# A gMLP mixer's seven products: where the low parts are made and when the additions are issued

## The chip, the cores and the metric

The kernel runs on one core of a Trainium2 chip. The metric is the device time of one execution in microseconds, given as the median of several runs.

## The reference

A trunk of two layers over 512 frames of 1024 channels in float32. Each layer is a half-step SwiGLU FFN, a mixer, a second half-step FFN and a gated input embedding; each step is followed by a LayerNorm. Layer 0's mixer is an mLSTM, layer 1's is the gMLP of which this document speaks:

```python
def gmlp_mixer(x, w_in, b_in, vn_g, vn_b, ws, bs, w_out):
    B, S, _ = x.shape
    NB = S // GM_BLOCK
    u, v = jnp.split(jax.nn.gelu(x @ w_in + b_in, approximate=False), 2, axis=-1)
    v = layer_norm(v, vn_g, vn_b).reshape(B, NB, GM_BLOCK, GM_GROUPS, GM_GDIM)
    blk = jnp.arange(GM_BLOCK) // CHUNK
    mask = blk[:, None] >= blk[None, :]
    ws_m = jnp.where(mask, ws, jnp.zeros((), ws.dtype))
    s = jnp.einsum('gts,bnsgc->bntgc', ws_m, v) + bs.T[:, :, None]
    return (u * s.reshape(B, S, GM_WIDTH)) @ w_out
```

u and v have 2048 columns each. The part that the change touches computes v: 512 frames by 1024 channels times 1024 x 2048 weights, GELU, and the statistics of v's LayerNorm.

## The kernel before

**Three matmuls per product.** Every float32 operand is split in two: a high part, rounded to fp32r, and a low part, the rest. A product is three matmuls (high x high, low x high, high x low): lines L432, L433 and L434 (`mm3`).

**Weights.** The class `Weights` (W) has one list of weight tiles, in the order in which PE takes them, each 128x1024. `load` brings raw weights from HBM over SP's queue (L265) into raw slots; two half-size loads can share a slot, a "box". `fill` goes down the list as far as tiles of the next one's kind ("main": four, "extra": two) are free, and makes the high part on ACT (L311) and the low part in one of two ways: on DVE by a subtraction (L318), or, for the forms named in `by_dma`, by a negated copy on ACT (L306) to which POOL's queue adds the source by an accumulating DMA (L307). `release` gives a tile's place back, at once (and fills) or, with `later=True`, into a list `held` from which `refill(n)` takes n. Fills are thus issued at the places in the program where `release` and `refill` stand. The list order, and with it each engine's instruction order, is written out by hand; an engine takes its instructions strictly in that order and waits where an operand or a buffer isn't ready. A new tile in a buffer waits for every use of the old one, also for uses that stand further down in the program.

**v's columns** are made in chunks of 512. Chunk 2 is plain: `plain(2)` goes over four blocks of 128 tokens, each 24 matmuls into one PSUM bank (`gvps`), then DVE adds the bias (L1756), ACT applies GELU (L1716) and DVE takes the statistics (L1720). Hooks in blocks 1 and 2 turn the last 256 tokens of the layer's input (transposes, xh on ACT, xl on DVE, L705). Chunk 3 is done likewise at the end, `plain(3)`, with the scales of the LayerNorm.

**Chunks 0 and 1** together are done by a seven-product scheme (Strassen-Winograd) over halves of tokens and columns, in two halves of the inner dimension: products r = 0 to 6, each 24 matmuls, whose weights are seven forms:

```python
        made = [((b11[0],), as_loaded(b11)), ((b21[0],) if by_dma else (b12[0], b22[0], b21[0]), as_loaded(b21)), ((b12[0], b22[0]) if by_dma else (), t2),
                ((), t1), ((), as_loaded(b12)), ((), as_loaded(b22)), ((), as_loaded(b21))]
```

Form 2 (`t2`) and form 3 (`t1`) are sums made in place on DVE, `t2` of one sum after `t3`, which `sum_early` issues ahead, and `t1` of two (L134, L135); each stands twice, once for each half of the inner dimension. The other side's forms come from the input: u, w, y and z hold sums of token halves, `in_forms(r, f)` and `in_place(r, f)` split them for product r (the second in one buffer, tag "hp"). Products alternate between two pairs of PSUM banks, `banks[r % 2]`; `adds(r)` adds a pair to v on DVE (L1822) with the bias where it is the first, and must be done before product r + 2 starts, since that writes to the same pair. `adds(5)` and `adds(6)` also give the pairs back to `plain(3)`. `run_affine` finishes the LayerNorm before the mixer, for the residual: a multiplication on DVE (L820) and an accumulating DMA (L822), one for each of four token blocks. `load_spatial` loads `gm_ws` over ACT's queue (L1681); it is transposed on PE (L1691) after `plain(3)`'s first token block.

## Time and profile before

| what | us |
|---|---|
| median of 3 runs | 2194.47 (2193.58 to 2194.95) |
| the profiled execution's own time | 2195.17 |
| its span in the profile | 2193.3 |
| PE busy in the span | 2162.9 |
| first matmul of the chunk `plain(2)` | at 1488.1 |
| first matmul of the spatial sums, after `plain(3)` | at 1601.0 |

Times within the span are counted from its start. PE, PEld, DVE, ACT and POOL are TensorE's matmuls, its weight loads, VectorE, ScalarE and GpSimd; SPq, ACTq and POOLq are DMA issues. A row in order of time gives start and duration, the engine and the line, output <- inputs, and in brackets how long the engine had been idle and what ended that. A row of waits gives the total, the number of times and the longest.

### The profile page before, as it was taken

To read this page: it belongs to the slowest core of one execution; us is meant where nothing else is said; L and a number is where in the kernel's file an instruction comes from. 1 tells how busy PE (TensorE), PEld (TensorE's weight loads), DVE (VectorE), ACT (ScalarE), POOL (GpSimd) and SP (SyncE) were. 2 spreads that over 40 slices of the span, in tenths; PEclk is the share of its full clock that TensorE was granted. 3 is DMA by queue.
4 is the path that set the end of the run, shared out by engine and by line. 5 is a ranking of instruction groups with operands and counts; after the bars stand their busy time and mean duration, and the time that the engine had idled before them with its cause. 6 is when DMAs were issued, how large, how long until landed. Compare 5 with 4: busy or idle time off the path is not lost.

```text
span 2193.3 us, 33288 instructions
## 1 busy us (share of the span) xinstructions
PE 2162.9 (99%) x13085; PEld 1931.4 (88%) x13085; DVE 1775.8 (81%) x2551; ACT 1263.7 (58%) x1733; POOL 259.7 (12%) x315
## 2 busy tenths in 40 slices
PE   9999999999999999999999999998799999999998
PEld 8999998888888889999888999997688888999987
DVE  6988878777776789888878988887578788888887
ACT  4666656364646556666445666655555555666542
POOL 1111101020111111111001111100101101111100
PEclk9999999999999999999999999999899999999999
DMA  7787764375747487776536787753847738777651
GB/s 217 180 195 188 174 172 113 85 159 131 163 111 154 116 205 179 176 186 159 163 111 168 184 201 188 169 146 90 220 102 134 165 116 221 181 183 180 140 173 58
DMA packets 233478, 348.40 MB, mean 159 GB/s; under 512 B 9908, under 2 KB 164660, under 8 KB 233320
## 3 DMA queue, kind: packets, MB, share of 16 engines
q0 software_dynamic: 57408, 119.73, 32.3%
q1 hardware_dynamic: 169296, 211.83, 29.8%
q10 hardware_dynamic: 6616, 14.69, 2.0%
q8 instruction: 103, 1.69, 0.3%
q14 instruction: 55, 0.45, 0.1%
HBM read 224.58 MB, written 2.11 MB: 103 GB/s over the span
## 4 chain that ended last, share of the span: by engine, by line
PE 41%; DVE 4%; DMA 2%; ACT 2%; issue 2%; POOL 0%; SPq 0%; ACTq 0%; DVEq 0%; POOLq 0%
PE ups L434 5%; PE ups L433 5%; PE ups L432 5%; PE gps L432 4%; PE gps L433 4%; PE gps L434 4%; PE dps L432 1%; PE dps L434 1%; PE dps L433 1%; PE gups L432 1%; PE gups L433 1%; PE gups L434 1%; PE fps L434 1%; PE fps L432 1%; PE fps L433 1%
## 5 line engine op out<-in xcount | busy, mean ns | idle before, releaser
L311 ACT ACTIVATE whi<-wbox 128x1024 fp32r<-128x1024 f32 x266 | 278.7, 1053 | 231.2 <-DVE wbox L159 100.6
L433 PE MATMUL ups<-xl,whi 128*128 128x256 f32 x1152 | 326.0, 283 | 0.0
L434 PE MATMUL ups<-xh,wlo 128*128 128x256 f32 x1152 | 326.0, 283 | 0.0
L432 PE MATMUL ups<-xh,whi 128*128 128x256 f32 x1152 | 325.8, 283 | 0.0
L307 POOL DMA_DIRECT2D wlo<-wbox x160 | 136.0, 850 | 1000.5 <-ACT wlo L306 650.1
L432 PE MATMUL gps<-whi,fhi 128*128 128x512 f32 x644 | 252.9, 393 | 0.0
L433 PE MATMUL gps<-wlo,fhi 128*128 128x512 f32 x644 | 252.3, 392 | 0.0
L434 PE MATMUL gps<-whi,flo 128*128 128x512 f32 x644 | 251.5, 391 | 0.0
L311 ACT ACTIVATE whi<-wraw 128x1024 fp32r<-128x1024 f32 (+1 forms) x188 | 192.5, 1046 | 102.3 <-DVE wraw L135 22.6
L433 PEld LDWEIGHTS ups<-xl,whi 128*128 128x128 f32 x1152 | 220.6, 191 | 2.6
L432 PEld LDWEIGHTS ups<-xh,whi 128*128 128x128 f32 x1152 | 220.6, 191 | 2.6
L434 PEld LDWEIGHTS ups<-xh,wlo 128*128 128x128 f32 x1152 | 220.6, 192 | 0.0
L831 DVE TENSOR_TENSOR xt<-xt,gps 128x512 f32<-128x512 f32 x302 | 195.6, 682 | 28.8 <-PE gps L434 28.6
L306 ACT ACTIVATE wlo<-wbox 128x1024 fp32r<-128x1024 f32 x160 | 167.2, 1045 | 11.4 <-DVE wbox L167 11.4
L318 DVE TENSOR_TENSOR wlo<-wraw,whi 128x1024 fp32r<-128x1024 f32 (+1 forms) x111 | 132.6, 1213 | 47.7 <-ACT whi L311 46.9
L311 ACT ACTIVATE whi<-wquarter 128x1024 fp32r<-128x1024 f32 (+1 forms) x140 | 135.2, 966 | 58.6 <-ACT wlo L306 20.4
L434 PEld LDWEIGHTS gps<-whi,flo 128*128 128x128 f32 x644 | 120.9, 188 | 26.9
L432 PEld LDWEIGHTS gps<-whi,fhi 128*128 128x128 f32 x644 | 121.3, 188 | 22.0
L433 PEld LDWEIGHTS gps<-wlo,fhi 128*128 128x128 f32 x644 | 121.4, 188 | 21.3
L324 DVE TENSOR_TENSOR wlo<-wquarter,whi 128x1024 fp32r<-128x1024 f32 (+1 forms) x116 | 139.2, 1200 | 0.0
L1020 DVE TENSOR_TENSOR flo<-h,fhi 128x512 fp32r<-128x512 f32 (+1 forms) x140 | 89.0, 636 | 46.1 <-ACT fhi L1017 45.8
L324 DVE TENSOR_TENSOR wlo<-wbox,whi 128x1024 fp32r<-128x1024 f32 x92 | 112.2, 1219 | 0.0
(413 smaller groups left out, 5826.9 us busy)
## 6 DMA issues: line engine op xcount, KB each, us to landing
wlo<-wbox POOLq DMA_DIRECT2D x160, 512.0 KB, 5.6
wbox<-in_ffn_wgu_dram SPq DMA_DIRECT2D x144, 512.0 KB, 4.9
wquarter<-in_ffn_wd_dram SPq DMA_DIRECT2D x64, 512.0 KB, 6.5
wraw<-in_ml_w_in_dram SPq DMA_DIRECT2D x24, 1024.0 KB, 5.9
wlo<-wraw POOLq DMA_DIRECT2D x48, 512.0 KB, 6.5
wraw<-in_gm_w_in_dram SPq DMA_DIRECT2D x11, 1024.0 KB, 6.6
wraw<-in_ffn_wgu_dram SPq DMA_DIRECT2D x17, 512.0 KB, 5.6
wraw<-in_ffn_wd_dram SPq DMA_DIRECT2D x8, 1024.0 KB, 5.5
```

The source lines that it names most:

```text
L306: self.nc.scalar.activation(lo[:, s], src[:, s], AF.Copy, scale=-1.0)
L307: self.nc.gpsimd.dma_start(lo[:, s], src[:, s], accum_op=OP.add)
L311: self.nc.scalar.activation(hi[:, s], src[:, s], AF.Copy)
L318: self.nc.vector.tensor_sub(lo[:, s], src[:, s], hi[:, s].bitcast(F32))
L324: self.nc.vector.tensor_sub(lo, src, hi.bitcast(F32))
L432: mm(ps, st[0], mv[0], start=start, stop=False, skip_group_check=more)
L433: mm(ps, st[0], mv[1], start=False, stop=False, skip_group_check=more)
L434: mm(ps, st[1], mv[0], start=False, stop=stop, skip_group_check=more)
L831: vec.tensor_add(dst, dst, ps)
L1020: vec.tensor_sub(lo, src, hi.bitcast(F32))
```

## The change

- Form 0's low parts are also made by accumulating DMA, and for all of these forms the negated copy goes ahead of the high part.
- Ahead of `plain(2)`, all loads that have room are issued and `fill` runs, so that both tiles of form 0 are made there.
- In `plain(2)`: after block 0 the sums of z and y; after block 1 `sum_early` and, by `form_ahead(4, True)`, both sums `t2`; after block 2 the input's sums and three held statistics; in block 3 the splits for product 2, a refill and the high part of the input of product 3. Three tiles are released at once there, where it was two.
- Within the products, after the first half of product r: `adds(r - 1)` stands first, and behind it form sums, refills, splits, statistics and affine steps. Both sums `t1` stand in a row behind `adds(0)`. Tiles are released later and taken back by `refill`.
- The affine steps move from products 2 to 5 to products 4, 5 (two) and 6; `load_spatial` moves from the end of product 5 into product 6, behind its refill; chunk 3's bias load moves into product 5. The statistics of chunks 0 and 1 move behind later additions, the last ones behind `adds(6)`.

```diff
-V_BY_DMA = (1, 4, 5, 6)
+V_BY_DMA = (0, 1, 4, 5, 6)
...
+        self.neg_first.update(made[r][1] for r in by_dma)
         return [(kind, js, make) for js, make in made]
...
-                if by_dma and make in self.sums:
+                neg_first = make in self.sums or make in self.neg_first
+                if by_dma and neg_first:
                     negated()
                 self.nc.scalar.activation(hi[:, s], src[:, s], AF.Copy)
...
-                if by_dma and make not in self.sums:
+                if by_dma and not neg_first:
                     negated()
...
-    def form_ahead(self, n):
+    def form_ahead(self, n, now=False):
...
-                if self.loaded_at[j] > self.clock - 2:
+                if not now and self.loaded_at[j] > self.clock - 2:
                     return
...
-                if c >= 2:
+                if c == 3:
                     stats()
+                elif c == 2:
+                    held_stats.append(stats)
                 return stats
...
-                    W.release(later=len(given) >= (2 if c < 3 else 1))
+                    W.release(later=len(given) >= (3 if c < 3 else 1))
...
             def first_tokens():
-                W.sum_early()
                 for e, s in enumerate(halves):
                     vec.tensor_add(z[e], *(a[:, s].bitcast(F32) for a in quarters[0]))
-
-            def more_tokens():
                 vec.tensor_add(y, *(a.bitcast(F32) for a in quarters[1]))
 
+            def weight_sums():
+                W.sum_early()
+                W.form_ahead(4, True)
+
...
             def in_place(r, f):
                 both = hpool.tile([P, 2, 4, 256], F32R, name="x_s", tag="hp")
                 for s, src in f:
-                    split(both[:, 0, s], both[:, 1, s], src)
-                left[r] = both[:, 0], both[:, 1]
+                    sca.activation(both[:, 0, s], src, AF.Copy)
+                left[r] = both[:, 0], both[:, 1]
+
+                def low():
+                    for s, src in f:
+                        vec.tensor_sub(both[:, 1, s], src, both[:, 0, s].bitcast(F32))
+                return low
...
-            ahead = lambda: W.form_ahead(4)
-            plain(2, vbs[0], (((), (first_tokens,)), ((), (more_tokens,)),
-                              ((sums,), (lambda: W.form_ahead(4),)), ((lambda: in_forms(2, z),), ())))
-            banks, add, stats = [], lambda: None, lambda: None
+            while W.load():
+                pass
+            W.fill()
+            third_low = []
+            plain(2, vbs[0], (((), (first_tokens,)), ((), (weight_sums,)), ((), (sums, lambda: [held_stats.pop(0)() for _ in range(3)])),
+                              ((lambda: in_forms(2, z), W.refill, lambda: third_low.append(in_place(3, [(slice(0, 4), w)]))), ())))
+            banks = []
...
-                return take(j, (2 * i, 2 * i + 1)) if r in (1, 4, 5, 6) else lambda: None
+                return lambda: take(j, (2 * i, 2 * i + 1))
...
-                    if k == 0 and r:
-                        stats()
-                        stats = adds(r - 1)
-                    W.release()
-                    if r == 1 and k == 0:
-                        in_place(3, [(slice(0, 4), w)])
-                    elif r == 1:
-                        fourth_sum()
+                    if k == 0:
+                        if r == 0:
+                            new_v(0)
+                        elif r == 1:
+                            adds(0)
+                            W.form_ahead(2)
+                            W.refill(2)
+                            third_low[0]()
+                        elif r == 2:
+                            gelus = adds(1)
+                            in_forms(4, [u[:, s] for s in halves])
+                            held_stats.append(gelus())
+                            fourth_sum()
+                            new_v(1)
+                        elif r == 3:
+                            adds(2)
+                            in_place(5, list(zip(halves, z)))()
+                            held_stats.pop(0)()
+                        elif r == 4:
+                            adds(3)
+                            held_stats.pop(0)()
+                            run_affine(1, True)
+                        elif r == 5:
+                            held_stats.append(adds(4)())
+                            W.refill(2)
+                            next_vb = load_bias(3)
+                            run_affine(2, True)
+                        else:
+                            held_stats.append(adds(5)())
+                            W.refill(2)
+                            load_spatial()
+                            held_stats.pop(0)()
+                            run_affine(1, True)
+                    W.release(later=True)
+                    if k == 1 and r in (1, 2, 3):
                         W.refill(2)
                 W.clock += 2
-                if r in (0, 2):
-                    new_v(r // 2)
-                if r == 2:
-                    in_forms(4, [u[:, s] for s in halves])
-                elif r == 3:
-                    in_place(5, zip(halves, z))
-                elif r == 5:
-                    load_spatial()
-                    next_vb = load_bias(3)
-                if 2 <= r <= 5:
-                    run_affine(1, True)
-            stats()
-            adds(6)()
+            last = adds(6)()
+            for stats in held_stats:
+                stats()
+            last()
             new_v(3)
```

More of the change, by code (lines that the diff above doesn't have):

```diff
@@ L68, in __init__ @@
         self.boxes, self.rank, self.loaded_at, self.clock = [], {}, {}, 0
-        self.lent, self.early = None, []
+        self.lent, self.early, self.neg_first = None, [], set()
         self.hold, self.limit, self.ahead, self.forced, self.sums = False, None, False, False, set()
@@ L1712, in load_bias @@
                 return vb
+            held_stats = []
             def take(c, ts):
```

## The prediction

> **What bounds the kernel now.** I read the page first, then who PE waited for, then a table of stages around the change, then the engines' instructions in order of time.
>
> ```profile
> span 2193.3 us, 33288 instructions
> PE 2162.9 (99%) x13085; PEld 1931.4 (88%) x13085; DVE 1775.8 (81%) x2551; ACT 1263.7 (58%) x1733; POOL 259.7 (12%) x315
> ...
> PE gvps L432 <- DVE gvf L1822: 12.8, 3, 7.9
> PE gvps L433 <- DMA wlo<-wbox: 2.8, 1, 2.8
> PE gvps L434 <- DVE xl L705: 1.8, 1, 1.8
> PE gvps L432 <- DVE gvf L1756: 1.0, 1, 1.0
> ```
>
> TensorE sets the time: the kernel ends when PE has worked through its list, so only PE's waits and its clock can be won. The four lower rows are PE's waits (total, times, longest) in the gMLP's v: 18.4 us. The stages (length, PE busy, PEld, DVE, ACT, POOL, granted clock, DMA share, GB/s):
>
> ```profile
> 1512.00:1532.00 20.00, 16.14 (x57) 12.43 (x56) 16.79 (x21) 9.21 (x12) 1.72 (x2) 0.83 0.28 53
> 1532.00:1551.00 19.00, 14.24 (x49) 10.85 (x47) 11.44 (x15) 14.83 (x18) 4.89 (x6) 0.82 0.60 138
> 1551.00:1568.00 17.00, 16.60 (x72) 13.44 (x72) 8.92 (x11) 4.96 (x7) 2.77 (x4) 1.00 1.06 236
> 1568.00:1584.00 16.00, 8.38 (x27) 6.68 (x28) 11.94 (x16) 6.36 (x8) 0.85 (x1) 0.68 1.08 314
> 1584.00:1601.00 17.00, 17.00 (x81) 14.18 (x80) 8.56 (x19) 7.21 (x11) 1.11 (x2) 1.00 0.12 41
> ```
>
> Three stages have a clock well under 1, and the DMA engines are full from 1551 to 1584. PE in order of time:
>
> ```profile
> 1502.78 0.50 PE L434 MATMUL gvps<-whi,xl 128*128 128x512 f32 x1 [1.80 <-DVE xl L705]
> ...
> 1516.38 0.50 PE L432 MATMUL gvps<-whi,xh 128*128 128x512 f32 x1 [1.03 <-DVE gvf L1756]
> ...
> 1523.81 0.80 PE L433 MATMUL gvps<-wlo,xh 128*128 128x512 f32 x1 [2.82 <-DMA wlo<-wbox]
> ...
> 1532.01 0.39 PE L432 MATMUL gvps<-whi,fhi 128*128 128x512 f32 x1
> ...
> 1537.22 0.39 PE L434 MATMUL gvps<-whi,flo 128*128 128x512 f32 x1
> 1540.83 0.77 PE L432 MATMUL gvps<-whi,x_s 128*128 128x512 f32 x1 [3.22 <-DVE gvf L1822]
> 1541.40 0.63 PE L433 MATMUL gvps<-wlo,x_s 128*128 128x512 f32 x1
> ...
> 1546.52 0.62 PE L433 MATMUL gvps<-wlo,x_s 128*128 128x512 f32 x1
> ...
> 1551.14 0.47 PE L432 MATMUL gvps<-whi,fhi 128*128 128x512 f32 x1 [1.68 <-DVE gvf L1822]
> ...
> 1575.62 0.77 PE L432 MATMUL gvps<-whi,xh 128*128 128x512 f32 x1 [7.88 <-DVE gvf L1822]
> ```
>
> From 1532.01 to 1537.22 are the 24 matmuls of product r=2: 23 steps, 0.227 us each, so a product takes 5.44 us. After the wait of 3.22 the step is (1546.52 - 1541.40) / 12 = 0.427 us. That happens after the waits of 2.82, 3.22 and 7.88 us, and not after 1.80, 1.68 or 1.03: PE's clock halves for some 14 matmuls, 14 x 0.20 = 2.8 us each time, 8.4 in all. So 18.4 + 8.4 = 26.8 us is what a change here can win: a floor of 2195.2 - 26.8 = 2168.4 in the profiled execution's time (2195.17 us, 0.7 above the median of the three runs and 1.9 above its span).
>
> **Why PE waits.** DVE takes its list in order, and the additions that free a bank stand behind fills.
>
> ```profile
> 1499.70 1.23 DVE L122 TENSOR_TENSOR wbox<-wbox 128x1024 f32<-128x1024 f32 x1 [1.86 <-DMA wbox<-in_gm_w_in_dram]
> ...
> 1540.00 1.28 DVE L1822 TENSOR_TENSOR gvf<-gvps,gvf 128x512 f32<-128x512 f32 x2
> ...
> 1570.19 2.36 DVE L318 TENSOR_TENSOR wlo<-wraw,whi 128x1024 fp32r<-128x1024 f32 x2 [8.57 <-ACT whi L311]
> 1572.47 1.22 DVE L820 TENSOR_TENSOR xt<-xt,gb 128x1024 f32<-128x1024 f32 x1
> 1573.61 1.28 DVE L1720 BATCH_NORM_STATS2 gst<-gvf 128x6 f32<-128x512 f32 x2
> 1574.80 1.27 DVE L1822 TENSOR_TENSOR gvf<-gvps,gvf 128x512 f32<-128x512 f32 x2
> ```
>
> The 7.88 us are the clearest: product 5's sums (1574.80) stand behind two low parts of the last chunk, an affine step and two statistics, and the low parts wait for the chunk's second load:
>
> ```profile
> 1569.11 1.06 ACT L311 ACTIVATE whi<-wraw 128x1024 fp32r<-128x1024 f32 x1 [6.82 <-DMA wraw<-in_gm_w_in_dram]
> 1569.27 0.95 ACTq L1681 DMA_DIRECT2D wst<-in_gm_ws_dram  x2
> ```
>
> **The change, part by part.** The prices, for tiles of 128x1024 made from the boxes:
>
> ```profile
> L311 ACT ACTIVATE whi<-wbox x14: 1039/1043/1061, 1508.6 to 1549.6; 128x1024 fp32r<-128x1024 f32 x14
> L306 ACT ACTIVATE wlo<-wbox x8: 1040/1041/1046, 1517.8 to 1550.5; 128x1024 fp32r<-128x1024 f32 x8
> L307 POOL DMA_DIRECT2D wlo<-wbox x8: 841/854/1189, 1519.2 to 1551.9; - x8
> L318 DVE TENSOR_TENSOR wlo<-wbox,whi x6: 1217/1223/1226, 1509.7 to 1537.7; 128x1024 fp32r<-128x1024 f32 x6
> ...
> DMA to landing us min/median/max: 4.6/7.6/11.9
> ...
> q0 software_dynamic: 416, 1.51, 105.8%
> ```
>
> The landing row is that of wlo, the last that of 1545 to 1552.2: 1.51 MB, 2.9 accumulations, filled 7.2 us x 1.058, so one takes 2.65 us of all 16 engines.
>
> *Form 0 by DMA, filled ahead of the first chunk.* DVE loses 2 x 1.22; ACT gains 2 x 1.04 and makes its 4 x 1.04 = 4.2 us some 20 us earlier, before its first GELU; POOL gains two issues of 0.85, queued behind the norm's power. Product 0 comes over 13 us later, a landing takes at most 11.9: nothing on the path. Their accumulations collide with the last box loads, of which the row at 1499.70 shows one late already (next part). That the low part is now made before the high one changes nothing in the count: the accumulation starts one ACT pass, 1.04, sooner.
>
> *Weight sums one token block later, four instead of two.* y's sum (1.2) goes ahead, the four sums (4 x 1.2 = 4.8) now stand on DVE ahead of the low parts of the last token block, behind which PE's fourth block waits. The old wait of 1.80 goes with its cause; the new one is between 0 (ends about when PE arrives) and 1.8 (the same sums on the same load). I take 1.0, the middle, since the collision makes the load later.
>
> *Sums after the bias addition, statistics held.* The sums (as much as three tiles, 3 x 1.22 = 3.7 us of DVE) move behind the addition of block 2, so the 1.03 goes. The statistics, 0.64 each, fill DVE's later gaps; the next reader of st is the last chunk. Zero; without cover, eight of them would be 5 us of DVE.
>
> *Three releases in place of two, a refill and in_forms ahead.* Form 1's low parts are issued from about 1511 and 1513 and land by 1519 (7.6 at most counted); product 1 starts at about 1518.6, and its second half at 1521.3. The 2.82 and its clock go.
>
> *Additions ahead of fills.* Without waits product 0 starts at 1516.38 - 1.03 - 6 x 0.227 - 1.8 + 1.0 = 1513.2 (that row is its seventh matmul), 1 at 1518.6, 2 at 1524.1, 3 at 1529.5. DVE, full until then, goes from product 0's end: additions 1.3, four sums of form 3 4.9, two lows 2.4, the third input's low 1.2, additions 1.3 = 11.1, from about 1518.9 to 1530.0. Before, the second additions began at 1540.00. Product 3 waits 0.5 (between 0 and the 3.22 of its row); both fourth sums now stand behind.
>
> *Products 4 to 6.* ACT copies the high parts of form 3 once DVE has its sums (by 1524.7, above), to 1525.7; then it negates and copies form 4's two tiles, 4 x 1.04 by 1529.8, and the issues on POOL end at about 1527.5 and 1529.5. Form 5 follows the next input's copies and two GELUs, after the additions at 1530.0: 1533.6 and 1535.5. Form 6 follows the copies of in_place(5), which wait for product 3's end, 1535.4: 1538.5 and 1540.4. Their users start at 1535.4, 1540.9 and 1546.3, the second halves 2.7 later. So a landing may take 7.3 to 8.7 us. The median above is 7.6, and the spacing of 1.9 to 4 is looser than what one accumulation takes, 2.65, on most steps: I take 0.5 in all (0 to 4, from the 11.9). The copies of in_place(5) and in_forms(4) wait on ACT for the running product, and fills and GELUs queue behind them; DVE's low parts, one statistic and additions 3 follow 4.3 us after product 3, and product 5 needs them after 5.4: covered by 1.1.
>
> *The last chunk's second load.* Its slot comes free when form 5's first low part has landed, about 1539.5:
>
> ```profile
> q0 software_dynamic: 782, 2.88, 87.7%
> q1 hardware_dynamic: 548, 1.06, 18.5%
> ...
> wraw<-in_gm_w_in_dram SPq DMA_DIRECT2D x2, 1024.0 KB, 16.9
> ...
> wst<-in_gm_ws_dram ACTq DMA_DIRECT2D x2, 256.0 KB, 6.9
> ```
>
> The first three rows are of 1552.2 to 1569, the last of 1569 to 1576: a load beside a full software queue got 18.5% and landed after 16.9. The queue then holds four accumulations (form 5's second, form 6's two, one affine), 4 x 2.65 / 0.877 = 12.1 us, so to about 1552, of which the load gets some 2.3 of the 3.1 us of engines it needs (18.5% of 16.8); the load lands near 1553, its tile is ready at 1555.2, PE wants it at 1552.3 + 2.7 = 1555.0. I take 0.5 (0 to 4). Product 5's additions now stand ahead of these fills, so the 7.88 goes.
>
> *The spatial weights' load.* New wait: it stood behind product 5; now it stands on ACT behind the refill of product 6, so behind the late load's copies. Issued at 1554, landed 6.9 later, 1560.9; PE transposes these weights right after the last chunk's first token block, 1557.9. Wait 3.0, and since 2.82 was enough for the clock, 2.8 more. Bounds: 0 (landing in 3.9) to 6 + 2.8.
>
> The Trainium skill ("TensorE: Matmul & The Clock Gate", Part 1) gives about 3.4 us of idleness before the clock halves. By that this wait would be free of the 2.8; the row with 2.82 shows a shorter one that was not.
>
> *Affine steps, the bias load, u's first fills.* The four affine steps (1.22 of DVE and an accumulation each) move from products 2 to 5 to products 4, 5, 5 and 6, on POOL's queue behind form 6's low parts in place of among them: that is what loosens the spacing above, and nobody needs them before the down product. Two of them stand ahead of product 5's additions, so those end at about 1550.2; their bank is wanted by the last chunk at 1552.3: zero, with 2 us of cover. The two extra tiles come free with the last chunk's first blocks, so u's first two fills (2 x 1.04 of ACT, 2 x 1.22 of DVE) move there, into a stage where DVE had 8.56 of 17: zero.
>
> **Sum.** 26.8 - (1.0 + 0.5 + 0.5 + 0.5 + 3.0 + 2.8) = 18.5 won; 2195.2 - 18.5 = 2176.7 profiled, 2176 against the median.
>
> **Rivals.**
> - All covered: loads get half of the engines beside the software queue. At half, its 3.1 us of engines take 6.2 and it lands near 1547, the copies no longer wait, and the spatial load is issued at about 1552.5 behind product 5's GELUs: the 0.5, half of the 3.0 and the 2.8 go, 2171, and 2168 if the first waits go too. Against: the 87.7 to 18.5 above. 0.12. The Trainium skill ("DMA: Bandwidth & Descriptors", Queues, rings and completion order) states such a turn between queues, packet by packet; the trace's shares are far from even.
> - The software queue is the bound: landings of 11.9 and 16.9. Product 4 waits 4.0 + 2.8; form 5 lands at 1545.5, the load at 1562.4, ready 1564.7, wanted 1561.7: 3.0 + 2.8; with 1.5 from above 14.1 lost, 2182. For it: DMA share 1.06. 0.22.
> - Slower: ACT and DVE become a convoy. The copies that wait for the running product hold all behind them; once DVE is over 1.1 late, each step waits, and from 2.8 the clock falls too, 5.6 a step. Five of the steps after product 2 eat 28 of the 26.8: with 1.5, 2197. Against: DVE 11.44 of 19. 0.06.
> - No change: it is given back after the last chunk, where two fills of u now stand before the scales. Against: 1584 to 1601, PE is full with DVE at 8.56 of 17. 2194. 0.06.
>
> **How the numbers follow.** My forecast has 0.50, the rest, 0.04, lies between it and no change. Under 0.2% (4.4 us) this measurement can't tell from nothing. Faster: 0.50 + 0.12 + 0.22 + 0.04 = 0.88; same 0.06; slower 0.06. The range goes from half of the covered case to the second rival with the upper ends of the first two waits (0.8 + 2.7) and a part of a clock loss, 2169 to 2187; the forecast's own is 2171 to 2181.
>
> **What would show it.** PE's waits for L1822 and wlo gone or under 1 us, product 3 starting near 1530, the last chunk near 1552; one wait of the spatial weights' transposes for wst, with slow matmuls behind. Wrong if the products 3 to 6 show waits over 2.8 us, or PE waits for whi of the last chunk by more than 4.

## The result, and the profile after

The changed kernel takes **2179.47 us** (median of 4 runs, 2178.55 to 2181.65) against 2194.3 (2193.58 to 2194.95) for the kernel before: ratio 0.9934, 95% interval [0.9917, 0.9951]. It is faster by about 15 us; 2176 was forecast, in a range of 2169 to 2187. The profiled execution took 2179.92 us, 15.25 less than the one before.

In the changed file the lines are shifted: a product's three matmuls are L434 to L436, the high part is L313, the negated copy L307, its DMA L308, VectorE's low part L320, the additions L1837, the last chunk's bias addition L1762, the load of the spatial weights L1683 and their transposes L1693.

The head of the page, and PE's waits from 1485 to 1600 us (total, times, longest):

```profile
span 2178.0 us, 33294 instructions
PE 2158.9 (99%) x13085; PEld 1929.2 (89%) x13085; DVE 1772.0 (81%) x2549; ACT 1265.6 (58%) x1735; POOL 264.1 (12%) x317
...
PE wsps L1693 <- DMA wst<-in_gm_ws_dram: 3.2, 2, 1.7
PE gvps L434 <- ACT whi L313: 2.9, 1, 2.9
PE gvps L435 <- DVE wlo L320: 0.8, 1, 0.8
PE gvps L435 <- DMA wlo<-wbox: 0.7, 1, 0.7
```

All four waits of before are gone: no product waits for a bank (L1837 isn't among the releasers), and the fourth token block doesn't wait for xl. PE's busy time is nearly the same, 2158.9 against 2162.9; what shrank are waits and slow matmuls. Two losses are new, both behind a late load: the last chunk's weights (PE waits for the high part whi and right behind it for the low part wlo) and the spatial weights (wst, which PE transposes into the bank wsps). The stages after (length, PE, PEld, DVE, ACT, POOL, granted clock, DMA share, GB/s):

```profile
1512.00:1528.00 16.00, 16.00 (x72) 13.27 (x71) 15.88 (x19) 10.37 (x13) 1.65 (x3) 1.00 0.37 62
1528.00:1551.00 23.00, 22.26 (x98) 17.79 (x97) 16.32 (x23) 15.37 (x21) 6.56 (x8) 1.00 1.04 238
1551.00:1567.00 16.00, 9.17 (x33) 6.51 (x32) 9.42 (x13) 4.46 (x6) 0.86 (x1) 0.84 1.10 297
1567.00:1586.00 19.00, 19.00 (x76) 15.50 (x75) 10.06 (x22) 7.87 (x12) 1.66 (x3) 0.86 0.47 161
```

Up to 1551 PE is full at full clock, though DVE is full beside it (15.88 of 16.00). What is still lost lies in the last two rows, where PE has 9.17 of 16 and a clock of 0.84 and 0.86. PE there, in order of time:

```profile
1556.91 0.50 PE L434 MATMUL gvps<-whi,xh 128*128 128x512 f32 x1 [2.87 <-ACT whi L313]
1558.17 0.54 PE L435 MATMUL gvps<-wlo,xh 128*128 128x512 f32 x1 [0.76 <-DVE wlo L320]
...
1561.92 0.39 PE L435 MATMUL gvps<-wlo,xh 128*128 128x512 f32 x1
1562.14 0.40 PE L436 MATMUL gvps<-whi,xl 128*128 128x512 f32 x1
1564.00 0.66 PE L1693 MATMUL wsps<-ident,wst 128*128 128x128 f32 x4 [1.46 <-DMA wst<-in_gm_ws_dram]
1566.40 1.11 PE L1693 MATMUL wsps<-ident,wst 128*128 128x128 f32 x4 [1.75 <-DMA wst<-in_gm_ws_dram]
1567.17 0.78 PE L434 MATMUL gvps<-whi,xh 128*128 128x512 f32 x1
...
1572.31 0.40 PE L434 MATMUL gvps<-whi,xh 128*128 128x512 f32 x1
```

From 1558.17 to 1562.14 are 10 steps from one matmul to the next, which at 0.227 us, the step at full clock, would be 2.3 us: 1.7 lost. From 1567.17 to 1572.31 are 12 steps, 2.7 at full clock: 2.4 lost. So the last chunk loses 2.87 + 0.76 + 1.7 = 5.3 us on its weight and 1.46 + 1.75 + 2.4 = 5.6 us on the spatial weights. The first of these is the term that the prediction had at 0.5.

### The profile page after: what moved, and what is told of

It reads as the page before. It is cut to its first block, busy times and chain, and to the rows that moved or that the text cites. A ratio compares the mean times of both kernels' runs of the same rounds, so it can differ in the third digit from the quotient of the medians.

```text
span 2178.0 us, 33294 instructions
## 1 busy us (share of the span) xinstructions
PE 2158.9 (99%) x13085; PEld 1929.2 (89%) x13085; DVE 1772.0 (81%) x2549; ACT 1265.6 (58%) x1735; POOL 264.1 (12%) x317
## 4 chain that ended last, share of the span: by engine, by line
PE 42%; DVE 4%; DMA 2%; ACT 2%; issue 1%; POOL 0%; ACTq 0%; DVEq 0%; POOLq 0%; SPq 0%
PE ups L436 6%; PE ups L435 6%; PE ups L434 6%; PE gps L434 4%; PE gps L435 4%; PE gps L436 4%; PE gups L434 1%; PE gups L435 1%; PE gups L436 1%; PE dps L436 1%; PE dps L434 1%; PE dps L435 1%; PE fps L435 1%; PE fps L434 1%; PE fps L436 1%
## 5 line engine op out<-in xcount | busy, mean ns | idle before, releaser
L313 ACT ACTIVATE whi<-wbox 128x1024 fp32r<-128x1024 f32 x266 | 278.8, 1053 | 226.4 <-DVE wbox L160 100.6
L436 PE MATMUL ups<-xh,wlo 128*128 128x256 f32 x1152 | 326.0, 283 | 0.0
L434 PE MATMUL ups<-xh,whi 128*128 128x256 f32 x1152 | 325.7, 283 | 0.0
L308 POOL DMA_DIRECT2D wlo<-wbox x162 | 139.7, 862 | 986.0 <-ACT wlo L307 628.9
L434 PE MATMUL gps<-whi,fhi 128*128 128x512 f32 x644 | 252.9, 393 | 0.0
L436 PE MATMUL gps<-whi,flo 128*128 128x512 f32 x644 | 251.5, 391 | 0.0
L313 ACT ACTIVATE whi<-wraw 128x1024 fp32r<-128x1024 f32 (+1 forms) x188 | 192.5, 1045 | 97.8 <-DVE wraw L135 22.6
L434 PEld LDWEIGHTS ups<-xh,whi 128*128 128x128 f32 x1152 | 220.5, 191 | 2.6
L436 PEld LDWEIGHTS ups<-xh,wlo 128*128 128x128 f32 x1152 | 220.6, 192 | 0.0
L307 ACT ACTIVATE wlo<-wbox 128x1024 fp32r<-128x1024 f32 x162 | 169.4, 1045 | 11.3 <-DVE wbox L168 11.3
L320 DVE TENSOR_TENSOR wlo<-wraw,whi 128x1024 fp32r<-128x1024 f32 (+1 forms) x111 | 132.6, 1211 | 46.8 <-ACT whi L313 46.2
L313 ACT ACTIVATE whi<-wquarter 128x1024 fp32r<-128x1024 f32 (+1 forms) x140 | 135.2, 966 | 58.7 <-ACT wlo L307 20.4
L436 PEld LDWEIGHTS gps<-whi,flo 128*128 128x128 f32 x644 | 120.9, 188 | 27.0
L434 PEld LDWEIGHTS gps<-whi,fhi 128*128 128x128 f32 x644 | 121.3, 188 | 22.0
```

What stands on the lines that cost most here:

```text
L307: self.nc.scalar.activation(lo[:, s], src[:, s], AF.Copy, scale=-1.0)
L308: self.nc.gpsimd.dma_start(lo[:, s], src[:, s], accum_op=OP.add)
L313: self.nc.scalar.activation(hi[:, s], src[:, s], AF.Copy)
L320: self.nc.vector.tensor_sub(lo[:, s], src[:, s], hi[:, s].bitcast(F32))
L434: mm(ps, st[0], mv[0], start=start, stop=False, skip_group_check=more)
L436: mm(ps, st[1], mv[0], start=False, stop=stop, skip_group_check=more)
```

## The experiments

The kernel before took 2193.7 to 2195.3 us in the medians beside these runs, so differences between kernels below 1 us are left alone, unless their runs don't overlap.

**Where do these two losses come from?** Theory A: the last chunk's second load starts too late, because its slot waits for form 5's first low part, made by DMA. Theory B: the load starts early enough, but the accumulating DMAs of the software queue leave it too small a share. For the spatial weights one theory: they need only be loaded earlier.

*Form 5 on VectorE* (form5_dve)

```diff
-V_BY_DMA = (0, 1, 4, 5, 6)
+V_BY_DMA = (0, 1, 4, 6)
```

> Form 5 leaves V_BY_DMA: its two low parts are subtractions on DVE again, two accumulations and two ACT passes fewer. Theory A (start): the last chunk's second load is late because its slot comes free only when form 5's first low part has landed (issued at 1539.6, landed 16.1 later). Made on DVE that part is done near 1533, so the load starts some 6 us sooner beside one queue entry or two fewer and lands near 1546 to 1549: PE's wait for whi (2.9), for wlo (0.8) and the slow matmuls behind them go, the spatial weights wait for 0 to 2.5. Cost: 2.4 us of DVE ahead of the additions of product 2, so product 4 waits about 1.4 in place of 0.7. Sum: 4 to 9 us below the changed kernel, 2170 to 2175. Theory B (share): the load is late because the software queue takes the engines; started sooner it still lands after 1553, and the time stays within 2 us of 2179.

Measured: 2179.64 us (2179.31 to 2180.81), ratio 0.993 [0.9915, 0.9945], no change against the changed kernel, where A had 2170 to 2175. In order of time, and then the load's size and time from issue to landing, first in the changed kernel, then here:

```profile
1534.23 0.37 SPq L266 DMA_DIRECT2D wraw<-in_gm_w_in_dram  x1
...
1548.90 0.39 ACTq L1683 DMA_DIRECT2D wst<-in_gm_ws_dram  x1
1549.24 1.05 ACT L313 ACTIVATE whi<-wraw 128x1024 fp32r<-128x1024 f32 x1
...
1564.57 1.11 PE L1693 MATMUL wsps<-ident,wst 128*128 128x128 f32 x4 [8.30 <-DMA wst<-in_gm_ws_dram]
```

```profile
wraw<-in_gm_w_in_dram SPq DMA_DIRECT2D x1, 1024.0 KB, 16.1
...
wraw<-in_gm_w_in_dram SPq DMA_DIRECT2D x1, 1024.0 KB, 6.4
```

The load is issued at 1534.23 in place of 1539.60, and the last chunk's wait for its weight is gone: the slot was what held the issue. But it lands 15.1 us earlier, at 1540.6 in place of 1555.7, of which the earlier issue is only 5.4. The other 9.7 are a shorter way: the edit also takes two accumulations out of the queue, and the load is through before the affine steps' additions come. So this run changes start and share together. And the spatial weights, issued 7.0 us earlier than in the changed kernel (1548.90 against 1555.91), land 16.6 us after their issue in place of 9.0, and PE waits 8.30 for them. What one load gains, the next one loses.

*No accumulating DMA in the affine steps* (no_affine_dma). Three of the affine steps leave out the addition of their second vector, so three accumulations of 512 KB are missing from the queue.

```diff
-                            run_affine(1, True)
+                            run_affine(1, "none")    # product 4; product 5's two likewise: tensor_mul, no DMA
```

> Leaves out part of the computation: the accumulating DMA that adds the LayerNorm's bias to the residual in the three affine steps of products 4 and 5 is not issued; all else stays, the multiplications on DVE too. Theory B (share): with three accumulations (3 x 2.65 us of all engines) fewer beside it, the chunk's second load, still issued near 1539.6, lands 5 us or more sooner, by 1551; PE's wait for whi goes. Theory A (start): most of its delay is form 5's second and form 6's two accumulations ahead of it; it lands within 3 us of 1555.7. The profile of one execution decides: landing time of this load, PE's wait for whi.

Measured, one run: 2175.08 us. Its load, its copy and the spatial weights:

```profile
1539.42 0.37 SPq L266 DMA_DIRECT2D wraw<-in_gm_w_in_dram  x1
...
1550.34 1.06 ACT L313 ACTIVATE whi<-wraw 128x1024 fp32r<-128x1024 f32 x1 [1.19 <-DMA wraw<-in_gm_w_in_dram]
...
wst<-in_gm_ws_dram ACTq DMA_DIRECT2D x2, 256.0 KB, 7.0
```

Issued at the same time as in the changed kernel (1539.60), the load lands 10.8 us after its issue in place of 16.1, and the wait for the high part is gone; the spatial weights land in 7.0 and cost 0.8 in all. So B is right: with the start unchanged, fewer accumulations beside the load remove the wait for the weight. PE then reaches the spatial products early and waits 3.0 for VectorE there, a wait that comes back below.

The queues of the changed kernel over that load say how small the share was (packets, MB, share of 16 engines); the first two rows are of 1541 to 1545, the others of 1545 to 1556:

```profile
q0 software_dynamic: 220, 0.79, 100.0%
q1 hardware_dynamic: 48, 0.10, 7.3%
...
q0 software_dynamic: 426, 1.55, 72.3%
q1 hardware_dynamic: 613, 1.02, 27.0%
```

In that time POOL issues two more accumulations, those of product 5's affine steps:

```profile
1546.77 0.86 POOL L824 DMA_DIRECT2D xt<-gb  x1 [5.48 <-DVE xt L822]
1547.91 0.86 POOL L824 DMA_DIRECT2D xt<-gb  x1 [0.28 <-DVE xt L822]
```

Over the whole flight of the load, 1539.60 to 1555.7, the hardware queue had 20.0% of the engines: 22.0% up to 1552, and then 13.6% beside 95.9% for the software queue.

*The spatial weights ahead of the refill* (spatial_early)

```diff
                         else:
+                            load_spatial()
                             held_stats.append(adds(5)())
                             W.refill(2)
-                            load_spatial()
```

> load_spatial stands ahead of adds(5) and of the refill in product 6, nothing else moves. Theory A and B alike: the load of the spatial weights is issued when product 5 is done (1545.3) and not behind the late copy (1555.9), lands by about 1555, and PE's two waits for wst (3.2) go with the slow matmuls of 1567 to 1572 (12 x 0.2 = 2.4): 2174. Rival (lost to contention): its 0.5 MB take some 1.6 us of the DMA engines from the chunk's second load, which then lands up to 3 us later and PE waits that much longer for whi: 2176 to 2178.

Measured: 2181.78 us (2180.05 to 2182.61), ratio 0.9938 [0.9923, 0.9952]; not faster than the changed kernel, and above both forecasts. Its waits:

```profile
PE sps L1929 <- DVE rsum L1708: 3.9, 1, 3.9
PE gvps L434 <- ACT whi L313: 3.2, 1, 3.2
```

The wait for wst is gone and PE reaches the spatial sums at 1580.06, 5.9 us earlier than in the changed kernel (1585.96). Then a new wait of 3.9 and slow matmuls behind it take that back (the granted clock is 0.50 from 1597 to 1601): PE now comes to the spatial products before VectorE is through with v's scales. The row names rsum, which VectorE writes between the last scales and the first split.

**What holds the end of v?** The chain on VectorE from the last chunk's first bias addition to the first split behind the scales; before the change, then after:

```profile
1583.98 0.69 DVE L1756 TENSOR_TENSOR gvf<-gvps,gvb 128x512 f32<-128x512 f32 x1
...
1612.06 0.68 DVE L438 TENSOR_TENSOR gvh<-gvf,gvh 128x512 fp32r<-128x512 f32 x1
```

```profile
1565.06 0.67 DVE L1762 TENSOR_TENSOR gvf<-gvps,gvb 128x512 f32<-128x512 f32 x1
1566.43 0.69 DVE L1724 BATCH_NORM_STATS2 gst<-gvf 128x6 f32<-128x512 f32 x1 [0.70 <-ACT gvf L1720]
1567.38 1.23 DVE L320 TENSOR_TENSOR wlo<-wraw,whi 128x1024 fp32r<-128x1024 f32 x1 [0.25 <-ACT whi L313]
1568.52 0.26 DVE L1733 BATCH_NORM_AGGREGATE gmv<-gst 128x2 f32<-128x24 f32 x1
...
1595.85 0.68 DVE L440 TENSOR_TENSOR gvh<-gvf,gvh 128x512 fp32r<-128x512 f32 x1
```

It took 28.1 us before and takes 30.8 after: u's two low parts (1.23 and a wait of 0.25 each), which the prediction costed at nothing, stand between the statistics and the scales. In spatial_early it is 30.8 as well (1565.48 to 1596.25). So the chain starts later or earlier with the last product, but isn't shorter for a PE that is early.

*The scales ahead of u's refill, in spatial_early* (scales_early)

```diff
                     if c == 3:
+                        rest = scales(t)
                         if t < 2:
                             W.refill()
-                        rest = scales(t)
                         if t < TB - 1:
                             rest()
```

> The variant with the spatial weights loaded early (spatial_early), and in the last chunk the scales of a token block ahead of the refill of u's tiles, not behind it. In every variant so far the chain from the first bias addition of the last chunk to the first split behind its scales takes 30.8 us, 28.1 before the change; u's two low parts (1.23 each, with 0.25 of wait) stand in it. Theory of the chain: they belong beside it, in the stretch where VectorE waits for the power on GpSimd. The chain then takes about 28 us, the wait of 3.85 at the first spatial product shrinks to about 1, and with it goes at least a part of the slow matmuls behind it: 2177 to 2179 against 2181.8. Rival, total work: VectorE is simply full there, the low parts come as late at another place of its list, the chain keeps 30.8 and the wait its 3.8: 2181 to 2182.

Measured: 2176.9 us (2175.2 to 2178.09), ratio 0.992 [0.9905, 0.9935], 4.9 us less than spatial_early.

```profile
1563.12 0.68 DVE L1762 TENSOR_TENSOR gvf<-gvps,gvb 128x512 f32<-128x512 f32 x1
...
1566.88 0.15 DVE L1738 SCALAR_TENSOR_TENSOR grs<-gmv,grs 128x1 f32<-128x1 f32 x1
1566.95 1.22 DVE L320 TENSOR_TENSOR wlo<-wraw,whi 128x1024 fp32r<-128x1024 f32 x1
...
1591.19 0.69 DVE L440 TENSOR_TENSOR gvh<-gvf,gvh 128x512 fp32r<-128x512 f32 x1
```

The low part now follows the scales, and the chain takes 28.1 us again; the wait at the spatial products is 1.4 in place of 3.9. The rival, that VectorE is simply full there, falls. A part of the 4.9 us isn't the chain's. In the profiled executions the difference is 6.3, and 2.6 of it is there before the first spatial sums (1577.49 against 1580.06): the wait for the high part was 1.3 here and 3.2 in spatial_early, an early stage that the edit doesn't touch, and I have no cause for that.

*The same order in the changed kernel alone* (scales_alone)

> The changed kernel, with the scales ahead of u's refill as the only edit. There TensorE reaches the first spatial product at 1597.8, and the split that it needs begins at 1595.85, so the 2.7 us of low parts in the chain would be hidden. Theory: the chain shrinks to about 28.1 and the time stays, 2179 to 2180 (2179.5 for the changed kernel). Rival: the order costs the changed kernel something as well, by other places where VectorE is late: 2176 to 2178.

Measured: 2179.06 us (2178.26 to 2180.06), ratio 0.993 [0.9914, 0.9947]: the same as the changed kernel, as forecast. The chain takes 29.1 us there (1564.38 to 1593.49) and not 28.1, since VectorE now waits 1.05 and 0.39 for PE in it. So the 2.7 us were a wrong cost, but a hidden one there: PE was late by the two loads anyway.

**Which parts of the change carry the gain?**

*Product 5's additions behind the fills again* (adds5_last)

```diff
                         else:
-                            held_stats.append(adds(5)())
                             W.refill(2)
...
                             run_affine(1, True)
+                            held_stats.append(adds(5)())
```

> Product 5's additions go behind the refill, the statistics and the affine step in product 6, as they stood before the change. Forecast: DVE reaches them only after the late low parts (end near 1559.2), at about 1562 to 1563, so the last chunk's first block waits for its bank some 11 us from 1551 in place of 3.7 for its weights; the spatial load has landed by then, so the waits for wst and one of the two slow stretches go. Net 1 to 4 us slower than the changed kernel: 2180 to 2183. Rival: the late load alone sets the time, the order of the additions is worth nothing: within 1 us of 2179.

Measured: 2183.48 us (2181.84 to 2183.91), ratio 0.9944 [0.9927, 0.996].

```profile
1562.93 0.77 PE L434 MATMUL gvps<-whi,xh 128*128 128x512 f32 x1 [11.32 <-DVE gvf L1837]
```

The wait of the kernel before is back, larger (11.32 against 7.88). It costs only 4 us against the changed kernel, since the waits for the weight (2.87 + 0.76, with their slow matmuls) and for wst lie inside it. PE reaches the first spatial sums only 1.1 us later (1587.08); the rest is a new wait of 1.4 + 0.8 at the spatial products. So this order is worth 4 us alone, not 7.88 and its clock: the load that the fills wait for is just as late for PE itself.

*No fill ahead of the first chunk* (fill_late)

```diff
             while W.load():
                 pass
-            W.fill()
             third_low = []
```

> The changed kernel without the fill ahead of the first chunk: form 0 is filled at the last hook, in block 2, as it was before. Its four passes (4.2 us) then stand on ACT at about 1506 to 1510.5, ahead of form 1's, so form 1's low parts are issued at about 1514 and 1516 and land near 1519 and 1521; they are wanted at 1517.2 and 1519.9. Also the sums t2 stand behind form 0's reads on DVE. Forecast: PE waits 1.5 to 3 for form 1 and up to 1 more at product 3, 2 to 5 us slower than the changed kernel: 2181 to 2185. Rival: all of it is covered, as the landings take only 4.5 while the DMA engines are idle, and what is lost is won back at the late load, which then waits for less: within 1 us of 2179.

Measured: 2183.49 us (2181.16 to 2184.25), ratio 0.9949 [0.9935, 0.9962].

```profile
1521.98 0.50 PE L434 MATMUL gvps<-whi,xh 128*128 128x512 f32 x1 [2.67 <-DVE gvf L1762]
```

Form 0 is then made on ACT from 1506.17 on, the sums wait for its slots and stand on DVE ahead of the last block's bias addition (1521.24), and PE waits 2.67 for that bank with slow matmuls behind it. The forecast had the size, but with a wait for form 1's low parts. By the medians the early fill is worth 4.0 us; the profiled execution is the fastest of the four (2181.16, 1.2 above the changed kernel's), so the row doesn't account for all of it.

*Form 0's low parts on VectorE* (no_form0)

```diff
-V_BY_DMA = (0, 1, 4, 5, 6)
+V_BY_DMA = (1, 4, 5, 6)
```

> The changed kernel with form 0's low parts on DVE, made ahead of the first chunk: 2 x 1.14 us more on DVE at about 1495 to 1497, which is full from there to 1531. Forecast: the last token block waits some 0.7 for xl and product 3 some 1.2 for its bank, which was ready 0.1 to 0.2 ahead; PE's later wait for the late load shrinks by as much only if the load does not move with it, and it does, since the load waits for form 5: 1 to 2 us slower than the changed kernel, 2180 to 2182. Rival: no difference (within 1 us), since the 1.4 us gap on DVE before xl takes it up.

Measured: 2182.69 us (2182.25 to 2182.95), ratio 0.9947 [0.9931, 0.9962], 3.2 above the changed kernel. The wait for xl, which the prediction had put at 1.0 for the changed kernel and which is 0 there, is 1.3 here: the two low parts that VectorE is spared are what takes it away. With shorter holds just before it, PE is then 2.3 us behind the changed kernel (this matmul starts at 1509.09, there at 1506.75), and 2.4 at the first spatial sums.

**A version without both losses.**

*Spatial weights in u's buffer, loaded early, and statistics ahead* (spatial_in_u_stats)

```diff
-                wst2 = hpool.tile([P, 2, 2, 4, P], F32, name="wst", tag="hp")
+                wst2 = near.tile([P, 2, 4, P], F32, name="wst", tag="gvh")
...
                             new_v(1)
+                            load_spatial()          # product 2
...
                             held_stats.append(adds(5)())
-                            W.refill(2)
-                            load_spatial()
+                            held_stats.pop(0)()
                             held_stats.pop(0)()
                             run_affine(1, True)
+                            W.refill(2)
```

> Two moves. The spatial weights are loaded in product 2 into the buffer of u, which is free by then, so the load is over long before the transposes and adds nothing to the contended stretch. And in product 6 both pairs of statistics and the affine step go ahead of the refill, into the 8 us in which DVE waits for the late copies. Theory C (chain): after spatial_early what binds is not PE's wait for wst but the chain on DVE and ACT from the late low parts (1556.9) to the first gvh (1595.9 to 1596.5); PE's wait for wst hid it with 1.3 us to spare. Then this version takes 4 statistics and an affine step (2.4 + 1.1 = 3.5 us) off the chain, PE comes to the spatial products at about 1592 in place of 1597.8, gvh is ready at about 1593: 5 us below the changed kernel, 2173 to 2175. Rival: the chain is bound by ACT's part (scales, GELUs), then the time stays at spatial_early's, 2180 to 2182.

Measured: 2179.72 us (2179.05 to 2180.44), ratio 0.9933 [0.9921, 0.9946]: no gain, where 2173 to 2175 was expected. The waits for wst are gone, but the 0.5 MB now lie among the accumulations ahead of the weight's load, and PE waits 2.7 + 0.5 for it and 2.1 for low parts by DMA, and then 1.3 + 0.8 at the spatial products.

*The same with form 5 on VectorE* (spatial_in_u_stats_f5)

> The version before with form 5's low parts on DVE as well, so that the last chunk's second load starts at about 1534 and lands near 1549, as in form5_dve. Theory C with A: no wait for whi, the low parts of the last chunk at about 1553, the chain's first bias addition at about 1558 in place of 1565, gvh at about 1589: 8 to 9 us below the changed kernel, 2170 to 2172. Rival (contention): the spatial weights' 0.5 MB at 1531 make form 4's and 6's accumulations late, PE's waits for wlo grow to 2 or more and part of it is lost: 2173 to 2176.

Measured: 2175.55 us (2173.97 to 2177.12), ratio 0.9914 [0.9901, 0.9928], in the rival's range, though not by its waits: none for a low part by DMA is left, and none for a load.

*And the scales ahead of u's refill* (f5_scales)

> The same order of scales and refill in the fastest variant (spatial weights in u's buffer, statistics ahead, form 5 on VectorE), which took 2175.55 and waits 1.55 + 0.75 at the spatial products. Theory of the chain: these waits go, 2173 to 2174. Rival, total work: they stay, 2175 to 2176.

Measured: 2170.21 us (2169.75 to 2171.35), ratio 0.9891 [0.9876, 0.9906], 5.3 less where 1.6 to 2.6 was expected. Of PE's waits 1.55 + 0.75 at the spatial products 0.4 are left, 1.9 us. About another 1.5 is the clock. Both kernels wait about as long at product 4, behind additions that stand after form 5's low parts (they start at 1535.08 and 1535.28); the first two rows are of spatial_in_u_stats_f5:

```profile
1535.91 0.76 PE L434 MATMUL gvps<-whi,fhi 128*128 128x512 f32 x1 [2.19 <-ACT wlo L307]
1536.47 0.63 PE L435 MATMUL gvps<-wlo,fhi 128*128 128x512 f32 x1
```

```profile
1536.11 0.47 PE L434 MATMUL gvps<-whi,fhi 128*128 128x512 f32 x1 [2.07 <-DVE gvf L1837]
1536.42 0.39 PE L435 MATMUL gvps<-wlo,fhi 128*128 128x512 f32 x1
```

After 2.19 us the matmuls are slow, after 2.07 they are not. The forecast held for the waits; the clock's part is luck, since the edit doesn't touch product 4. The profiled executions differ by 3.6 us, the fastest of spatial_in_u_stats_f5 being the profiled one; the remaining 1.6 between the medians isn't in these two traces.

*And form 5 made behind the additions of product 2* (f5_scales_late)

```diff
                             adds(2)
+                            W.refill(2)
                             in_place(5, list(zip(halves, z)))()
...
-                    if k == 1 and r in (1, 2, 3):
+                    if k == 1 and r in (1, 3):
```

> As f5_scales, and form 5 made half a product later, behind the additions of product 2 and not ahead of them. Theory of the order: the one wait left in the products (2.19 at product 4, additions behind two low parts) goes and with it the slow matmuls (clock 0.93 over 23 us, 1.6 us), while the last chunk's second load is issued some 1.5 us later, at 1536 to 1537, and still lands before its tile is wanted: 2169 to 2171. Rival, the load: it meets the accumulations of form 6 and of an affine step again and lands 12 to 16 us later, with a wait for the high part of 2 us or more: 2172 to 2175.

Measured: **2169.36 us** (2169.21 to 2169.63), ratio 0.9886 [0.9869, 0.9902], the fastest of all and 10.1 below the changed kernel. All of PE's waits from 1485 to 1600:

```profile
PE sps L1932 <- DVE gvh L440: 0.8, 1, 0.8
PE gvps L435 <- DMA wlo<-wbox: 0.6, 1, 0.6
```

The expected 1.5 us of delay of the load didn't come (issued at 1534.76): VectorE had waited 1.30 us for the high parts in f5_scales, and the additions fill that gap. The spatial sums start at 1573.9, 27.1 us earlier than in the kernel before. The prediction had worked out 26.8 as the most that can be won, so that figure was a little too small.

## Why the prediction was right, and where it wasn't

Counted to the first matmul of the spatial sums (1600.99 before, 1585.96 after), the change won 15.0 us, of 18.5 forecast. By the prediction's own terms, in us:

| term | forecast | measured |
|---|---|---|
| waits and slow matmuls to be won | 26.8 | all of the old ones gone |
| fourth token block for xl | 1.0 | 0 |
| product 3 for its bank | 0.5 | 0 |
| low parts by DMA in products 4 to 6 | 0.5 | 0.7 |
| the last chunk's second load | 0.5 | 5.3 (2.87 + 0.76 + 1.7) |
| the spatial weights' load | 3.0 + 2.8 | 3.2 + 2.4 |
| left over | 18.5 | 26.8 - 11.6 = 15.2 |

- **What was right.** That PE's own list is the bound, with about 26.8 us of waits and slow matmuls in it (f5_scales_late won 27.1); that additions ahead of fills remove the waits for banks (adds5_last brings 11.32 of it back); that the next thing late are the two loads, in that order. Product 3 was forecast for 1530.0 and started at 1528.1; the load's issue for about 1539.5 and came at 1539.60.
- **The mis-sized term** is the last chunk's second load, put at 0.5 and measured at 5.3. The prediction gave the load 18.5% of the engines until the software queue's four accumulations were through at about 1552, and all of them after that, so that it landed near 1553. The share was about right: the hardware queue had 22.0% up to 1552. What failed is the end of the queue. Product 5's two affine steps, whose move the prediction put at zero because nobody needs them early, issued two more accumulations at 1546.77 and 1547.91, and from 1552 to 1555.7 the hardware queue had 13.6%. (Of the 1.11 MB that this queue moved in the flight, 1.05 are the load's, so u's loads behind it took little.) The load landed at 1555.7, 2.7 late; no_affine_dma, without these two and product 4's, lands it at 1550.2 (the two by themselves weren't measured). PE also came 1.0 earlier than counted, at 1554.04. The wait came to 2.87 + 0.76, inside the stated bounds of 0 to 4, and the slow matmuls behind it, 1.7, are a part that the term didn't hold.
- **Right by luck: the spatial weights' load.** 3.0 + 2.8 was forecast and 3.2 + 2.4 measured, but none of the parts is right. The load was issued at 1555.91 and not 1554, its two halves landed after 9.0 (median) and not 6.9, and PE wanted them at 1562.5 and not 1557.9, because the last chunk's weights had held it up. The slow matmuls were priced by a single wait of 2.82; they came behind two of 1.46 and 1.75.
- **Two waits that didn't come.** xl and product 3's bank were set at middle values between "0" and the old wait. Both came out at 0; no_form0 shows that the spared low parts were what decided the first.
- **u's first fills: not zero.** This is the place that the fourth rival named, at 0.06, and the reason given against it (VectorE at 8.56 of 17) doesn't hold. They lengthen the chain behind the last chunk from 28.1 to 30.8. The cover that the prediction named, VectorE's free time in the stage, was the wrong thing to look at: what counts is whether they stand in the chain to the spatial products. It was hidden only by the late loads (scales_alone: no change), and as soon as these were mended it cost 2.5 us of wait (3.9 against 1.4) and slow matmuls (spatial_early, scales_early).
- **The other rivals.** "Loads get half of the engines" is refuted for this load by 7.3% and 27.0%; in form5_dve, started ahead of the affine steps, the same load comes near to it (the hardware queue had 43.9% from 1534 to 1541). The Trainium skill ("DMA: Bandwidth & Descriptors", Queues, rings and completion order) has each engine take turns between queues by packet; the trace counts 220 packets against 48 in the 4 us from 1541, far from one for one, though no run here shows that what it counts are those packets. "The software queue is the bound" was half right: its price for the load, 3.0 + 2.8, is close to the 5.3 measured, while the low parts for the products came in time (8.5 us median, 0.7 of wait). The convoy didn't come: from 1512 to 1551 PE was busy 38.3 of 39 us.

## What to carry to other kernels

When a wait is removed, follow the loads that come behind it to their landing, and count beside each load every accumulating DMA that will be issued before it lands, also those of work that nobody waits for. The same 1024 KB landed after 6.4, 10.8 or 16.1 us here, by what was beside it. Work put into an engine's free time costs nothing only if it stands outside the chain that the next stage waits for; put the short, awaited instructions ahead of the fills. Repairs of one loss gave nothing here (form5_dve, spatial_early, spatial_in_u_stats: +0.2 to +2.3 us), since each exposed the next wait; together, with the new order of scales and form 5, they gave 10.1 us.

## What the runs showed of the hardware

- A wait of 2.19 us was followed by slow matmuls, one of 2.07 was not; 1.46 and 1.75 within 4 us were followed by 12 slow ones. The length of the waits doesn't decide alone: 1.37 + 0.75 at the spatial products was followed by a granted clock of 0.61 from 1593 to 1597 in scales_early, 1.55 + 0.75 by 1.00 in the same stretch of spatial_in_u_stats_f5. The Trainium skill ("TensorE: Matmul & The Clock Gate", Part 1) gives about 3.4 us of idleness; here less was enough.
- The two loads of the spatial weights, 256 KB each, landed after 7.0 us with three accumulations fewer (no_affine_dma), 8.0 when issued in product 2 (f5_scales_late), 9.0 in the changed kernel, 14.3 in spatial_early and 16.6 in form5_dve. Of the 16.6 I can't say which transfer held them: from 1548 to 1552 the hardware queue had 98.2% of the engines and the software queue 1.1%, so it wasn't the accumulations alone.
